# A hybrid decoder layer on one core: how its weight sums, its channel steps and the X of its recurrence are laid out

## Chip, cores and metric

One Trainium2 chip, one of its cores. The time is device microseconds of one execution of the program; the median of three runs of the kernel before is 2164.18 us (2163.83 to 2165.83). TensorE (PE) does the matmuls, VectorE (DVE) and ScalarE (ACT) the elementwise work, GpSimd (POOL) a little arithmetic and the issue of many DMAs, SyncE (SP) the issue of the loads.

## The reference

One decoder layer over 2048 tokens of width 1024, all in float32. A state-space branch and a sliding-window attention branch share one input projection; their outputs are normalised, concatenated and projected; a SwiGLU FFN of hidden width 2816 follows. Cut to what this change touches:

```python
# state-space branch: 32 groups of 16 channels, 64 complex states each
_, _, xr, xi = lax.associative_scan(_s5_combine, (a_re, a_im, bu_re, bu_im), axis=1)
y = (einsum('blgp,ghp->blgh', xr, c_re) - einsum('blgp,ghp->blgh', xi, c_im) + d * uf)
y = gelu(y.reshape(bsz, L, SSM_WIDTH))
...
# FFN
gu = rms_norm(h, g_pre_ffn) @ w_gate_up
ff = (silu(gu[..., :D_FF]) * gu[..., D_FF:]) @ w_down
h = h + rms_norm(ff, g_post_ffn)
```

## The kernel before

The layer runs in three phases: projection with the recurrence (to about 352 us), attention with the output projection (to about 799 us), and the FFN, which takes the rest. A planner orders the instructions of each engine ahead of time from priorities and its own estimate of durations; on the chip each engine then runs its list strictly in that order. Operations handed to `keep_in_program_order` (called `pin` in the channel steps) keep the place that the program gives them.

**Recurrence.** Time is cut into 256 chunks (NC) of 8 steps. `table_quad` (called for four quads) builds the matrices of the groups on chip and stores them in `tab_d`. `ssm_pair` (16 pairs of groups) loads its table `tab` and its input U, makes S with matmuls (L659: for each of two parts r, real and imaginary, and each group g2 of the pair, an output of 64 partitions), turns S into X on DVE (rotation, scan L672, rotation back) and computes Y = Toeplitz part (L686, from U) + state part (L687, from X); gelu (L689) and a store follow. Before, X is held as [part r in the upper or lower 64 partitions, group, chunk], so that four DVE operations of 64 partitions each write it, crossing partitions, and one Y bank takes, for each group, one matmul of 128 rows with U and one of 128 rows with X. Every float32 matmul of these is two instructions in the trace. The PSUM tag "pa" has four banks; S, Y and the transposes of V take theirs from it. The tiles tab have two buffers, those of U, X and y three. `weave` hands out about 0.9 pairs after each group of 24 matmuls of the Q, K and V projection (`qkv_stream`, tile ps_q).

**FFN.** Each half s of the tokens (1024) runs `ffn_gu` and then `ffn_down`. Both use a seven-product scheme for 2x2 blocks, which needs sums of blocks of the activations and of the weights. `gu_runs` gives 21 runs: the first does the column blocks 0 and 11 together, each later one does one block. A run has four steps q, each with some matmuls. After every second run `ff_operands` stores the products F4 and their sums (tile fxd, POOL, L1312 to L1318). F4 has one buffer.

**Weight sums.** `down_sums` is a generator of 48 DMAs on POOL from DRAM to DRAM (L1334, tile wsd, 512 KB each, some that add to what is there), pinned. During the first half, three are handed out at the end of each run.

**Channel steps.** `channel_steps(1, ...)` turns the rows of the second half around for its FFN: `load` (SP, tile hx), `scale` (ACT L1119, pinned), `turn` (eight transposes on PE, L1127, pinned), then in the second four of eight rows also two loads (tile hb) and `sums` (four DVE operations, the first pinned, and four stores, L1154). The tiles hx and hb share one buffer, ho has another. Before, 21 steps are handed out, one at the end of each run, and the load of row i+1 stands in the same step as the last use of row i:

```python
steps += [chain((scale, i)), chain((even, t), (load, i + 1))]
steps += [chain((scale, i)), chain((odd, t)), chain((sums, t), *([(load, i + 1)] if t < 3 else []))]
```

Of the kernel before, what the change touches and what calls it, by code (L numbers as in the profile page):

```python
# [9 lines left out]
F32 = mybir.dt.float32  # L10
# [3 lines left out]
AF = mybir.ActivationFunctionType  # L14
ALU = mybir.AluOpType
# [4 lines left out]
P = 128  # L20
# [11 lines left out]
NC = SEQ // T8  # L32
# [15 lines left out]
class Layer:  # L48
# [448 lines left out]
    def table_quad(self, q):  # L497

        nc, tp = self.nc, self.p_tab
        qs = slice(4 * q, 4 * q + 4)  # L500
        S4 = [P, 4, 16, 8]
        t1 = tp.tile(S4, F32, tag="qt1", name=f"qt1_{q}")
        t2 = tp.tile(S4, F32, tag="qt2", name=f"qt2_{q}")
        gr = tp.tile(S4, F32, tag="qgr", name=f"qgr_{q}")
        gi = tp.tile(S4, F32, tag="qgi", name=f"qgi_{q}")
        rr = self.rwr[:, qs, :].unsqueeze(2).to_broadcast(S4)
        ri = self.rwi[:, qs, :].unsqueeze(2).to_broadcast(S4)
        br = self.bb[:, 0, qs, :].unsqueeze(3).to_broadcast(S4)
        bi = self.bb[:, 1, qs, :].unsqueeze(3).to_broadcast(S4)
        self.cmul(gr, gi, rr, ri, br, bi, t1, t2)  # L510
        yield
        krev = self.bank([P, 4, 32], "krev")
        for i in range(4):
            nc.tensor.matmul(krev[:, i, :], gr[:, i].rearrange("p h j -> p (h j)"),
                             self.cbd[:, 0, 4 * q + i].rearrange("p g h -> p (g h)"), start=True, stop=False)
            nc.tensor.matmul(krev[:, i, :], gi[:, i].rearrange("p h j -> p (h j)"),
                             self.cbd[:, 1, 4 * q + i].rearrange("p g h -> p (g h)"), start=False, stop=True)
        out = tp.tile([P, 4, 768], F32, tag="tabout", name=f"tabout_{q}")
        for r, g in enumerate((gr, gi)):
            w = self.bank([P, 4, P], "ws")  # L520
            for i in range(4):
                nc.tensor.transpose(w[:, i, :], g[:, i].rearrange("p h j -> p (h j)"), self.ident)
            nc.scalar.copy(out[:, :, r * P:(r + 1) * P], w)
        kd = tp.tile([P, 8, 16], F32, tag="kd", name=f"kd_{q}")
        self.tt(kd, self.dmask.unsqueeze(1).to_broadcast([P, 8, 16]),
                self.d_in[:, 8 * q:8 * q + 8].unsqueeze(2).to_broadcast([P, 8, 16]), ALU.mult)
        self.tt(kd, kd, krev.rearrange("p a (g h) -> p (a g) h", g=2), ALU.add)
        yield
        for i2 in range(2):
            tb = self.bank([P, 4, P], "toep")  # L530
            for i in range(4):
                ii = i2 * 4 + i
                nc.tensor.matmul(tb[:, i, :], self.ext[:, ii, :],
                                 kd.rearrange("p g h -> p (g h)"), start=True, stop=True)
            for a in range(4):
                nc.scalar.copy(
                    out[:, a, 256:512].rearrange("p (g i) -> p g i", i=8)[:, :, i2 * 4:i2 * 4 + 4],
                    tb[:, :, a * 32:(a + 1) * 32].rearrange("p i g -> p g i"))
        fr = self.pwr[:, qs, 1:9].unsqueeze(2).to_broadcast(S4)
        fi = self.pwi[:, qs, 1:9].unsqueeze(2).to_broadcast(S4)  # L540
        cr = self.c_in[:, 0, qs, :].unsqueeze(3).to_broadcast(S4)
        ci = self.c_in[:, 1, qs, :].unsqueeze(3).to_broadcast(S4)
        ca = out[:, :, 512:768].rearrange("p q (g h i) -> p q g h i", g=2, h=16)
        self.tt(t1, fr, cr, ALU.mult)
        self.tt(t2, fi, ci, ALU.mult)
        for g2 in range(2):
            s = slice(g2 * 64, g2 * 64 + 64)
            self.tt(ca[0:64, :, g2], t1[s], t2[s], ALU.subtract)
        yield
        self.tt(t1, fr, ci, ALU.mult)  # L550
        self.tt(t2, fi, cr, ALU.mult)
        for g2 in range(2):
            s = slice(g2 * 64, g2 * 64 + 64)
            nc.vector.scalar_tensor_tensor(
                out=ca[64:128, :, g2].rearrange("p q h i -> p q (h i)"),
                in0=t1[s].rearrange("p q h i -> p q (h i)"), scalar=-1.0,
                in1=t2[s].rearrange("p q h i -> p q (h i)"), op0=ALU.mult, op1=ALU.subtract)
        nc.gpsimd.dma_start(self.tab_d[q][:, :, 0:768], out)
        yield

        E = tp.tile([P, 4, 2, NC], F32, tag="tabout", name=f"Etab_{q}")
        nc.scalar.copy(E[:, :, :, 0:64], self.E6[:, qs])
        for m in (64, 128):
            ng = self.tmp([P, 4], tag="eng")
            self.ts(ng, E[:, :, 1, m - 1], -1.0, None, ALU.mult, ALU.bypass)
            for i in range(4):
                et = tp.tile([P, 2, P], F32, tag="et", name=f"et_{q}_{m}_{i}", bufs=2)
                nc.scalar.activation(et[:, :, :m], E[:, i, :, 0:m], AF.Copy, scale=E[:, i, 0, m - 1:m])
                nc.vector.scalar_tensor_tensor(out=E[:, i, 0, m:2 * m], in0=E[:, i, 1, 0:m], scalar=ng[:, i:i + 1],
                                               in1=et[:, 0, :m], op0=ALU.mult, op1=ALU.add)  # L570
                nc.vector.scalar_tensor_tensor(out=E[:, i, 1, m:2 * m], in0=E[:, i, 0, 0:m],
                                               scalar=E[:, i, 1, m - 1:m],
                                               in1=et[:, 1, :m], op0=ALU.mult, op1=ALU.add)
        nc.gpsimd.dma_start(self.tab_d[q][:, :, 768:1280], E.rearrange("p q r c -> p q (r c)"))
        yield
# [71 lines left out]
    def ssm_pair(self, pr):  # L647
        nc = self.nc
        m, r0 = pr // 4, (pr % 4) * 32
        tab = self.s_tab.tile([P, 1280], F32, tag="tab", name=f"tab_{pr}")  # L650
        nc.sync.dma_start(tab, self.tab_d[m][:, pr % 4, :])
        U = self.s_u.tile([P, 2, NC], F32, tag="U", name=f"U_{pr}")
# [21 lines left out]
        b1 = self.s_z.tile(sh, F32, tag="a1", name=f"b1_{pr}")  # L674
        b2 = self.s_z.tile(sh, F32, tag="a2", name=f"b2_{pr}")
        self.tt(b1, z, erb, ALU.mult)
        self.tt(b2, z, eib, ALU.mult)
        X = self.s_u.tile([P, 2, NC], F32, tag="X", name=f"X_{pr}")
        nc.gpsimd.memset(X[:, :, 0:1], 0.0)
        for r, op in ((0, ALU.subtract), (1, ALU.add)):  # L680
            for g2 in range(2):
                s = slice(g2 * 64, g2 * 64 + 64)
                self.tt(X[r * 64:r * 64 + 64, g2, 1:NC], b1[s, r, 0:NC - 1], b2[s, 1 - r, 0:NC - 1], op)
        Y = self.bank([P, 2, NC], "Y")
        for g2 in range(2):
            nc.tensor.matmul(Y[:, g2, :], tab[:, 256 + g2 * P:384 + g2 * P], U[:, g2, :], start=True, stop=False)  # L686
            nc.tensor.matmul(Y[:, g2, :], tab[:, 512 + g2 * P:640 + g2 * P], X[:, g2, :], start=False, stop=True)  # L687
        y = self.s_u.tile([P, 2, NC], F32, tag="y", name=f"y_{pr}")
        nc.scalar.activation(y, Y, AF.Gelu_apprx_tanh)  # L689
        nc.scalar.dma_start(self.yT_d[m][r0:r0 + 32].rearrange("(g h) i c -> (h i) g c", g=2), y)  # L690


# [413 lines left out]
    def channel_steps(self, s, xp, xtag, xbufs, op, otag, obufs, bank):  # L1106

        nc = self.nc
# [47 lines left out]
        def chain(*fs):  # L1156
            return lambda: [f(i) for f, i in fs]

        steps = [chain((load, 8 * s))]
        for t in range(4):  # L1160
            i = 8 * s + t
            steps += [chain((scale, i)), chain((even, t), (load, i + 1))]
        for t in range(4):
            i = 8 * s + 4 + t
# [58 lines left out]
    def ffn_gu(self, s):  # L1223
        nc, tc = self.nc, self.tc
        with ExitStack() as c:
# [11 lines left out]
            for n, fs in enumerate(self.gu_runs()):  # L1237
                if fs[0] < NJ:
                    j = fs[0]
                    F4 = ff.tile([P, 4, TB], F32, tag="f4", name=f"f4_{s}_{j}")  # L1240
                groups = [self.gu_group(s, f, F4, ev) for f in fs]
                for q in range(4):
                    for g in groups:
                        self.gu_ahead()
                        next(g, None)
                    if fs[-1] == NF - 1 and q > 1:
                        self.got.append(self.down_operands(s, 0, q - 2))
                if fs[-1] >= NJ:
                    self.ff_operands(s, j, F4)
                if s == 0:  # L1250
                    for _ in range(3):
                        next(sums, None)
                    if side and n > 0:
                        side.pop(0)()
                    if n == 0:
                        side.pop(0)()
            for f in side:
                f()

    def gu_ahead(self):  # L1260

# [289 lines left out]
```

## Time and profile before

| | |
|---|---|
| median of 3 runs | 2164.18 us |
| profiled execution | 2163.8 us |
| its span (first to last instruction) | 2162.0 us |
| mean granted TensorE clock | 0.974 of full |
| PE busy | 2017.5 us (93%) |
| DVE busy | 1388.7 us (64%) |
| ACT busy | 924.4 us (43%) |
| POOL busy | 301.3 us (14%) |

PE is busy for most of the span, so time is to be had only where PE waits or runs at less than its full clock, or by giving it less to do. Busy shares are averages over stages; the stages around the change are read one by one. Idle time printed behind an instruction is that of its engine just before it, with what ended it.

### The profile page before, as it was taken

How to read it: one execution, taken by the hardware profiler on the slowest of the kernel's cores; microseconds unless marked ns; L12 is line 12 of the kernel's file. 1: busy time of each engine (PE TensorE's matmuls, PEld its weight loads, DVE VectorE, ACT ScalarE, POOL GpSimd, SP SyncE). 2: the span in 40 equal slices, each digit the busy share in tenths (PEclk: the TensorE clock that was granted, in tenths of full speed). 3: DMA queues.
4: the chain of work that ended last, by engine and by line, in shares of the span. 5: the costliest groups of instructions: out<-in, count | busy, mean ns of one | idle time of the engine just before them, and what ended most of it. 6: DMA issues, size and time to landing. Idle time of an engine off the chain costs nothing. (4 is left out here: it accounts for less than half of the span.)

```text
span 2162.0 us, 25798 instructions
## 1 busy us (share of the span) xinstructions
PE 2017.5 (93%) x9200; PEld 1635.8 (76%) x9200; DVE 1388.7 (64%) x2199; ACT 924.4 (43%) x1469; POOL 301.3 (14%) x655
## 2 busy tenths in 40 slices
PE   7998987999999798999979999999899999999997
PEld 5777665887877686778768777887688888887885
DVE  7876887887676747565456565446766656554446
ACT  6433114976565454333233344435333333334443
POOL 3211000112223431212112110001000000000001
PEclk9999998999899999999999999999999999999998
DMA  8566656534246744667566466656423222256664
GB/s 280 209 229 204 187 151 180 153 101 154 81 152 202 265 156 162 243 173 221 161 200 171 165 244 219 191 192 229 161 103 127 93 107 103 83 175 224 204 195 175
DMA packets 177425, 379.73 MB, mean 176 GB/s; under 512 B 32864, under 2 KB 53856, under 8 KB 177104
## 3 DMA queue, kind: packets, MB, share of 16 engines
q1 hardware_dynamic: 138112, 259.89, 37.6%
q0 software_dynamic: 32512, 109.79, 15.5%
q10 hardware_dynamic: 6672, 8.40, 1.3%
q8 instruction: 72, 1.18, 0.2%
q14 instruction: 57, 0.47, 0.1%
HBM read 281.87 MB, written 119.21 MB: 186 GB/s over the span
## 5 line engine op out<-in xcount | busy, mean ns | idle before, releaser
L220 PE MATMUL ps_gb<-bh,wh 128*128 128x512 f32 x704 | 279.4, 398 | 14.6 <-ACT f L1289 7.4
L222 PE MATMUL ps_gb<-bh,wl 128*128 128x512 f32 x704 | 275.6, 393 | 8.7 <-DVE wl L172 8.7
L221 PE MATMUL ps_gb<-bl,wh 128*128 128x512 f32 x704 | 277.0, 393 | 0.0
L222 PE MATMUL ps_dn<-wh_d,wl_x 128*128 128x512 f32 x616 | 244.3, 398 | 8.1 <-DVE wl_x L172 6.1
L220 PE MATMUL ps_dn<-wh_d,wh_x 128*128 128x512 f32 x616 | 243.6, 395 | 6.0 <-ACT wh_x L1091 4.2
L221 PE MATMUL ps_dn<-wl_d,wh_x 128*128 128x512 f32 x616 | 243.4, 395 | 1.1 <-DVE wl_d L172 1.1
L220 PEld LDWEIGHTS ps_gb<-bh,wh 128*128 128x128 f32 x704 | 133.3, 190 | 51.6 <-ACT f L1289 10.4
L222 PEld LDWEIGHTS ps_gb<-bh,wl 128*128 128x128 f32 x704 | 133.1, 189 | 39.4 <-DVE wl L172 10.0
L221 PEld LDWEIGHTS ps_gb<-bl,wh 128*128 128x128 f32 x704 | 133.1, 189 | 28.2 <-DVE bl L172 0.2
L220 PE MATMUL ps_gc<-bh,wh 128*128 128x512 f32 x352 | 139.8, 398 | 13.0 <-ACT wh L171 10.6
L171 ACT CAST wh<-fr 128x1024 fp32r<-128x1024 f32 (+1 forms) x88 | 73.5, 835 | 171.8 <-issue 87.9
L222 PEld LDWEIGHTS ps_dn<-wh_d,wl_x 128*128 128x128 f32 x616 | 117.7, 192 | 36.6 <-DVE wl_x L172 8.9
L220 PEld LDWEIGHTS ps_dn<-wh_d,wh_x 128*128 128x128 f32 x616 | 117.9, 191 | 32.2 <-ACT wh_x L1091 5.5
L172 DVE TENSOR_TENSOR wl_x<-xr,wh_x 128x1024 fp32r<-128x1024 f32 x72 | 81.6, 1133 | 92.4 <-ACT wh_x L171 92.4
L222 PE MATMUL ps_gc<-bh,wl 128*128 128x512 f32 x352 | 139.2, 396 | 0.5 <-DVE wl L172 0.5
L221 PE MATMUL ps_gc<-bl,wh 128*128 128x512 f32 x352 | 139.3, 396 | 0.0
L221 PEld LDWEIGHTS ps_dn<-wl_d,wh_x 128*128 128x128 f32 x616 | 117.8, 191 | 26.1 <-DVE wl_d L172 1.6
L172 DVE TENSOR_TENSOR wl_d<-dr,wh_d 128x1024 fp32r<-128x1024 f32 x84 | 95.1, 1132 | 61.1 <-ACT wh_d L171 61.1
L171 ACT CAST wh_x<-xr 128x1024 fp32r<-128x1024 f32 x72 | 70.7, 982 | 123.2 <-PE ps_dn L221 116.2
L171 ACT CAST wh_d<-dr 128x1024 fp32r<-128x1024 f32 x84 | 82.4, 981 | 91.1 <-PE ps_dn L221 64.0
L76 DVE TENSOR_TENSOR q<-ps_ga,q 128x512 f32<-128x512 f32 x44 | 30.3, 689 | 111.9 <-PE ps_ga L222 111.5
L172 DVE TENSOR_TENSOR wl<-sb,wh 128x1024 fp32r<-128x1024 f32 x44 | 53.8, 1222 | 61.5 <-ACT wh L171 61.5
(368 smaller groups left out, 4624.6 us busy)
## 6 DMA issues: line engine op xcount, KB each, us to landing
fr<-in_w_gu SPq DMA_DIRECT2D x88, 512.0 KB
xr<-fxd SPq DMA_DIRECT2D x70, 512.0 KB
dr<-wsd SPq DMA_DIRECT2D x40, 512.0 KB
fxd<-f POOLq DMA_DIRECT2D x22, 768.0 KB, 4.8
gwr_o<-in_w_out SPq DMA_DIRECT2D x64, 256.0 KB
wsd<-in_w_down POOLq DMA_DIRECT2D x30, 512.0 KB, 10.3
dr<-in_w_down SPq DMA_DIRECT2D x30, 512.0 KB
raw<-in_xT SPq DMA_DIRECT2D x56, 256.0 KB
```

The source lines that it names most:

```text
L76: (eng or self.nc.vector).tensor_tensor(out=out, in0=a, in1=b, op=op)
L171: nc.scalar.copy(hi, x)
L172: nc.vector.tensor_tensor(out=lo, in0=x, in1=f32(hi), op=ALU.subtract)
L220: t.matmul(out, wh, mh, start=first, stop=False, skip_group_check=more)
L221: t.matmul(out, wh, ml, start=False, stop=False, skip_group_check=more)
L222: t.matmul(out, wl, mh, start=False, stop=last, skip_group_check=more)
```

## The change

Three edits. In `table_quad` and `ssm_pair` X and its matrix are held by groups: the partitions are those of the states (group, state), and the free axis has the part r. Two DVE operations of 128 partitions write X; Y gets a bank for each group, with one matmul of 128 rows from U and two matmuls of 64 rows (partitions 0 to 63 for the first group, 64 to 127 for the second) from X; gelu runs once for each bank. In `ffn_gu` one weight sum goes out after step q = 0, one after q = 2 and one at the end of a run; the channel steps are handed out at q = 1 and q = 3 of all runs but the first. In `channel_steps` of the second half a load is a step of its own with an empty step behind it, and so is `odd`: 40 steps in place of 21.

```diff
         qs = slice(...)                       # table_quad
-        ca = out[:, :, 512:768].rearrange("p q (g h i) -> p q g h i", g=2, h=16)
+        ca = out[:, :, 512:768].rearrange("p q (r h i) -> p q r h i", r=2, h=16)
-        for g2 in range(2):
-            s = slice(g2 * 64, g2 * 64 + 64)
-            self.tt(ca[0:64, :, g2], t1[s], t2[s], ALU.subtract)
+        self.tt(ca[:, :, 0], t1, t2, ALU.subtract)
...
-        for g2 in range(2):
-            s = slice(g2 * 64, g2 * 64 + 64)
-            nc.vector.scalar_tensor_tensor(out=ca[64:128, :, g2]..., in0=t1[s]..., scalar=-1.0, in1=t2[s]...)
+        nc.vector.scalar_tensor_tensor(out=ca[:, :, 1]..., in0=t1..., scalar=-1.0, in1=t2...)
...
         for r, op in ((0, ALU.subtract), (1, ALU.add)):     # ssm_pair
+            self.tt(X[:, r, 1:NC], b1[:, r, 0:NC - 1], b2[:, 1 - r, 0:NC - 1], op)
+        Y = [self.bank([P, NC], "Y") for _ in range(2)]
+        for g2 in range(2):
+            nc.tensor.matmul(Y[g2], tab[:, 256 + g2 * P:384 + g2 * P], U[:, g2, :], start=True, stop=False)
+        for r in range(2):
             for g2 in range(2):
                 s = slice(g2 * 64, g2 * 64 + 64)
-                self.tt(X[r * 64:r * 64 + 64, g2, 1:NC], b1[s, r, 0:NC - 1], b2[s, 1 - r, 0:NC - 1], op)
-        Y = self.bank([P, 2, NC], "Y")
+                nc.tensor.matmul(Y[g2], tab[s, 512 + r * P:640 + r * P], X[s, r, :], start=False, stop=r == 1)
+        y = self.s_u.tile([P, 2, NC], F32, tag="y", name=f"y_{pr}")
         for g2 in range(2):
-            nc.tensor.matmul(Y[:, g2, :], tab[:, 256 + g2 * P:384 + g2 * P], U[:, g2, :], start=True, stop=False)
-            nc.tensor.matmul(Y[:, g2, :], tab[:, 512 + g2 * P:640 + g2 * P], X[:, g2, :], start=False, stop=True)
-        y = self.s_u.tile([P, 2, NC], F32, tag="y", name=f"y_{pr}")
-        nc.scalar.activation(y, Y, AF.Gelu_apprx_tanh)
+            nc.scalar.activation(y[:, g2], Y[g2], AF.Gelu_apprx_tanh)
...
+        if s:                                                # channel_steps
+            steps = []
+            for t in range(4):
+                i = 8 * s + t
+                steps += [chain((load, i)), chain(), chain((scale, i)), chain((even, t))]
+            for t in range(4):
+                i = 8 * s + 4 + t
+                steps += [chain((load, i)), chain(), chain((scale, i)), chain((odd, t)), chain(), chain((sums, t))]
+            return steps
...
+                    if q % 2 == 0:                           # ffn_gu, in the loop over q
+                        next(sums, None)
+                    elif side and n > 0:
+                        side.pop(0)()
                 if fs[-1] >= NJ:
                     self.ff_operands(s, j, F4)
-                if s == 0:
-                    for _ in range(3):
-                        next(sums, None)
-                    if side and n > 0:
-                        side.pop(0)()
-                    if n == 0:
-                        side.pop(0)()
+                next(sums, None)
             for f in side:
                 f()
+            for _ in sums:
+                pass
```

## Rows read from the trace of the kernel before

**Rows 1.** The page, busy time of the engines, share of the span, instructions.

```profile
PE 2017.5 (93%) x9200; PEld 1635.8 (76%) x9200; DVE 1388.7 (64%) x2199; ACT 924.4 (43%) x1469; POOL 301.3 (14%) x655
```

**Rows 2.** Waits of PE, 850 to 1265 us: total, times, longest.

```profile
PE ps_gc L220 <- ACT wh L171: 8.2, 1, 8.2
PE ps_gb L220 <- ACT f L1289: 7.4, 5, 2.8
PE ps_gb L220 <- ACT wh L171: 3.9, 3, 1.4
```

**Rows 3.** Stretches: length, busy PE, PEld, DVE, ACT, POOL, granted clock, DMA.

```profile
200.00:352.00 152.00, 127.34 (x563) 91.09 (x561) 127.42 (x239) 27.26 (x53) 12.47 (x35) 0.94 0.59 170
...
280.00:290.00 10.00, 10.00 (x50) 7.71 (x49) 9.87 (x20) 1.85 (x5) 0.10 (x1) 1.00 0.40 124
```

**Rows 4.** Groups of DVE, 200 to 352 us: busy, mean ns, idle before.

```profile
L76 DVE TENSOR_TENSOR X<-b,b 64x255 f32<-64x255 f32 x64 | 26.8, 419 | 1.6
L76 DVE TENSOR_TENSOR a<-ps_S,tab 128x512 f32<-128x512 f32 x32 | 21.1, 686 | 18.2 <-PE ps_S L659 17.9
...
L76 DVE TENSOR_TENSOR a<-a,a 128x256 f32<-128x256 f32 x32 | 12.1, 419 | 0.3
```

**Rows 5.** Groups of PE in the same stretch.

```profile
L659 PE MATMUL ps_S<-U,tab 128*64 128x256 f32 x128 | 22.0, 427 | 19.3 <-DMA U<-uTd 6.6 <-issue 6.3 <-DMA tab<-tabd 6.2
L687 PE MATMUL ps_Y<-X,tab 128*128 128x256 f32 x64 | 21.7, 424 | 4.8 <-DVE X L76 4.7
```

**Rows 6.** Timeline of one pair: start us, us, engine, line, operation.

```profile
250.32 0.39 PE L220 MATMUL ps_q<-xs,wh 128*128 128x512 f32 x1
...
250.77 1.08 PE L659 MATMUL ps_S<-U,tab 128*64 128x256 f32 x8
251.60 1.73 DVE L76 TENSOR_TENSOR X<-b,b 64x255 f32<-64x255 f32 x4
...
251.78 0.70 PE L686 MATMUL ps_Y<-U,tab 128*128 128x256 f32 x2
...
253.53 0.60 PE L686 MATMUL ps_Y<-U,tab 128*128 128x256 f32 x2
...
253.97 0.59 PE L687 MATMUL ps_Y<-X,tab 128*128 128x256 f32 x2
...
258.07 1.73 DVE L76 TENSOR_TENSOR X<-b,b 64x255 f32<-64x255 f32 x4
```

**Rows 7.** Groups of ACT, 200 to 352 us.

```profile
L689 ACT ACTIVATE y<-ps_Y 128x512 f32<-128x512 f32 x16 | 9.6, 598 | 65.9 <-PE ps_Y L687 61.0 <-DMA yTd<-y 4.9
...
L619 ACT COPY qe<-ps_q 128x512 f32<-128x512 f32 x6 | 3.5, 586 | 24.2 <-PE ps_q L222 12.2 <-DMA qd<-qe 9.8 <-DMA kd<-qe 2.2
```

**Rows 8.** The tile tabout, its DVE writes: ns min/median/max, first and last start.

```profile
L76 DVE TENSOR_TENSOR tabout<-qt,qt x8: 674/684/691, 89.5 to 174.6; 64x512 f32<-64x512 f32 x8
```

**Rows 9.** Timeline around the longest wait of the FFN's first half.

```profile
1111.99 2.50 POOL L1334 DMA_DIRECT2D wsd<-wsd  x5
1112.44 0.33 SPq L1116 DMA_DIRECT2D hx<-hd  x1
...
1127.22 1.15 ACT L1119 ACTIVATE hx<-hx,rstd 128x1024 f32<-128x1024 f32 x1 [8.64 <-DMA wsd<-wsd]
```

**Rows 10.** Timeline of PE behind that wait.

```profile
1129.88 0.79 PE L220 MATMUL ps_gc<-bh,wh 128*128 128x512 f32 x1 [8.21 <-ACT wh L171]
...
1133.03 0.41 PE L222 MATMUL ps_gb<-bh,wl 128*128 128x512 f32 x1
1133.27 0.40 PE L220 MATMUL ps_gb<-bh,wh 128*128 128x512 f32 x1
```

**Rows 11.** Timeline around a later row of the channel steps.

```profile
1235.43 0.34 SPq L1116 DMA_DIRECT2D hx<-hd  x1
...
1242.35 1.15 ACT L1119 ACTIVATE hx<-hx,rstd 128x1024 f32<-128x1024 f32 x1 [2.81 <-DMA hx<-hd]
```

**Rows 12.** The stretch of the twenty later runs of the FFN's first half.

```profile
864.00:1270.00 406.00, 386.14 (x1694) 311.49 (x1693) 234.06 (x323) 137.62 (x185) 75.26 (x102) 0.99 0.63 188
```

More of the change, by code (lines that the diff above doesn't have):

```diff
@@ L551, in table_quad @@
         self.tt(t2, fi, cr, ALU.mult)
-        for g2 in range(2):
-            s = slice(g2 * 64, g2 * 64 + 64)
[L554 to L557, printed above, removed]
+        nc.vector.scalar_tensor_tensor(
+            out=ca[:, :, 1].rearrange("p q h i -> p q (h i)"),
+            in0=t1.rearrange("p q h i -> p q (h i)"), scalar=-1.0,
+            in1=t2.rearrange("p q h i -> p q (h i)"), op0=ALU.mult, op1=ALU.subtract)
         nc.gpsimd.dma_start(self.tab_d[q][:, :, 0:768], out)
```

## The prediction

> **What bounds the kernel now.** The page comes first: PE is busy for 93% of the span, DVE for 64% [rows 1]. So a microsecond taken off DVE, POOL or a queue counts only where PE waits for it, and the question for each edit is which wait of PE stands behind it. The three edits touch two stages, which the waits of PE and the stretches take apart.
>
> The first half of the FFN (about 864 to 1270 us) is bound by PE, with few waits. From 850 to 1265 us the large ones are one of 8.2 us for a split of weights on ACT, five of together 7.4 us for a copy on ACT and three of together 3.9 us for splits again [rows 2]. The 8.2 us can be followed: POOL issued five weight sums within 2.5 us from 1111.99 on, SP issued a load hx at 1112.44, and ACT started the scaling of that row only at 1127.22, after 8.64 us in which it did nothing [rows 9]. The scaling is pinned, ACT runs in order, and the split that PE needed stood behind it. PE then began below its full clock: its eight matmuls from 1129.88 to 1133.03 took 3.15 us, where at the pace from 1133.03 to 1133.27 they take 1.9 [rows 10]. That is 1.2 us more.
>
> The recurrence (200 to 352 us, 16 pairs, 9.5 us each) has no single bound: PE and DVE are each busy for 127 of 152 us [rows 3]. Where DVE runs without gaps, one X follows the last by 6.47 us (251.60 to 258.07) [rows 6]. Nine of the fifteen 10-us stretches from 200 to 350 have DVE at 9.2 us or more, of which one is shown [rows 3]; in the others DVE waits for S, 17.9 us in all [rows 4], and PE for U, tab and issue, 19.1 us [rows 5]. tab is loaded again only when the Y of two pairs before is done, so this wait is a loop through X, Y and a load.
>
> **X by groups, DVE.** 64 writes of 64 partitions become 32 of 128. The old take 419 ns; so do operations of 128 partitions and 256 elements [rows 4], so the new are taken at 419 as well: 64 x 0.419 = 26.8 us become 13.4. If all of it shortens the stage it is -13.4. It is taken at the share of stretches that DVE fills, 9 of 15: -8.0 us. In the rest the waited-for load starts a little earlier too, which is counted at nothing.
>
> **X by groups, PE.** Per pair four instructions of 128 rows become eight of 64 rows; the Toeplitz part keeps four. The old pace is (253.97 - 253.53) / 2 = 0.22 us [rows 6], so 64 x 0.22 = 14.1 us now. No row has matmuls of 64 rows. The nearest is S, whose halves go to different partitions of the output: eight in 1.01 us (250.77 to 251.78), 0.126 each, so two run side by side there [rows 6]. By S: 128 x 0.126 = 16.1 us, +2.0. With no pair side by side: 128 x 0.22 = 28.2, +14.1. I take S, since the two groups use different rows and different banks.
>
> Going into S also costs: the matmul before starts 0.45 us ahead of it, where a full pace is 0.24 [rows 6, 10], so 0.2 us is lost. The new matmuls stand between ones of full height, two changes per pair, 32 x 0.22 = 7.0 us. Together +9.1 us of PE, between +2.0 and +21.1.
>
> The Trainium skill, page "TensorEngine Tiling (Array Packing)", section "Key Properties", says that changing the tiling mode drains the engine; the gap ahead of S agrees with it. The same section says that tiles work independently. By both rules the sum would be +9.1, without the first +2.0.
>
> PE idles for 25 of 152 us, which covers most of that. Only where PE is full as well does it lengthen the stage; that is so in three of the fifteen stretches, as in the one shown [rows 3]: 9.1 x 3/15 = +1.8 us. Without that cover it costs the 9.1. The stage gives -8.0 + 1.8 = -6.2 us, between -13.4 and about 0. Gelu in two pieces costs ACT a fixed part more; ACT is busy for 27 of 152 us [rows 3], so nothing.
>
> **The table.** Sixteen DVE writes of 64 partitions, 0.684 us [rows 8], become eight: 5.5 us of DVE over four quads, 1.4 each. Quads wait for their stores and, at the end, for an ACT copy that stood behind a store. Counted at nothing, at best -1.4 (the last quad).
>
> **Weight sums and channel steps.** Twenty runs take 406 us, 20.3 each, of which PE is busy for 386 [rows 12]. Work and number of DMAs stay; only the order changes. The sums come one at a time, some 5 to 10 us apart. A load of the channel steps moves from the step of the sums, where on SP it waits for the stores out of the same buffer, to half a run later, and keeps a whole run until its scaling. Behind it on SP stand weight loads, which lose a blocker. Between scaling and transposes half a run is left, 10 us; pinned transposes on PE would wait if ACT were later than that, but ACT is lightly used. The three sums that now go out in the first run pass POOL's stores of h and arithmetic there; nothing on PE waits for those for a whole run, so nothing, at most +2.
>
> With no burst in front, a load needs about what it needed at 1235.43, where the scaling followed at 1242.35, 6.9 us later [rows 11]; 20 us cover it. So the 8.2 and the 1.2 us go. The 2.81 us that ACT waited at 1242.35 cost PE the longest of the five copy waits, 2.8 us [rows 2, 11]; there the load was issued late, behind the stores, and half a run of distance removes that. The other four (7.4 - 2.8 = 4.6, with the 3.9 us of splits) come from the order on ACT, and may fall otherwise: I add one more such pair, 4.6/4 + 3.9/3 = +2.5 us. Sum: -8.2 - 1.2 - 2.8 + 2.5 = -9.7 us. Bounds: -12.2 without new waits, 0 if the waits only move.
>
> **Sum.** 2163.8 (profiled) - 6.2 - 9.7 = 2147.9 us. The profiled execution is 0.4 us below the median of the runs, so 2148 us.
>
> **The rivals.**
> *PE fills the recurrence.* If 64-row matmuls do not run side by side, PE gets +21.1 on 127.3 us, 148 of 152, and takes over as the bound: the stage stays, and 2163.8 - 9.7 = 2154. For it: no row shows such matmuls. Against: S.
> *The bursts stay.* The sums are pinned on POOL, in a list that also has stores waiting for DVE; a wait there can collect the single sums into a burst again, so that the edit doesn't do what it says. Then only the recurrence gains: 2163.8 - 6.2 = 2158. For it: three sums are handed out per run, yet five went in one stretch [rows 9]. Against: with one per step at most two should collect.
> *Neither gains*: both of these, 2164.
> *The banks run out (slower).* A pair takes three of the four "pa" banks instead of two, and a Toeplitz part made early holds them. If S of the next pair must wait for the gelu, DVE idles for every pair: X chain 6.47 - 0.84 = 5.6, Y 1.0, change 0.2, gelu 0.6 [rows 7], S 1.0, and the queue of PE ahead of S, say eight projection matmuls of 0.24 = 1.9: 10.3 us per pair, (10.3 - 9.5) x 16 = +13. ACT's waits for stores, 9.8 us at L619 [rows 7], then hold banks too. 13 + 9.8 - 9.7 = +13: 2177. It decides from 9.5 + 9.7/16 = 10.1 us per pair. For it: with Y made early, four banks leave no spare. Against: S waits for tab anyway, which comes after that Y.
> The skill's page on tiling, section "Restrictions and Gotchas", names the same pressure: row tiles write to different PSUM banks. No run here shows it yet.
>
> **How the numbers follow.** A measurement of this kernel can tell 0.2%, 4.3 us, from no change. The forecast has 0.45 (its own range 2140 to 2156), PE filling 0.18, bursts 0.12, neither 0.10, banks 0.15. Faster: 0.45 + 0.18 + most of 0.12 (0.09) = 0.72. Same: 0.03 + 0.10 = 0.13. Slower: 0.15. The range begins where both stages reach their best bound (-13.4 - 1.4 - 12.2 = -27: 2137) and ends at 2168, past "neither"; what lies beyond is most of the banks' 0.15.
>
> **What would show it.** X: 32 writes of 128x255 near 0.42 us. Y from X: 64-row matmuls at about 0.13 us from start to start (0.22 means the first rival). The last Y some 6 us earlier. The 8.2 us wait gone, no scaling waiting over 1 us, sums singly on POOL. S waiting for ACT's gelu, or pairs over 10.1 us, means the banks. The prediction is wrong if the planner, given other durations, moves waits elsewhere: attention and the second FFN half, which the edits don't touch, should be within 3 us.

## The result, and the profile after

The changed kernel is slower: 2179.95 us, median of six runs (2174.89 to 2184.96), against 2165.01 us for the kernel before (2163.37 to 2171.32); the ratio is 1.0066, 95% interval 1.0044 to 1.0087. The forecast was 2148 us with a range of 2137 to 2168. The profiled execution of the changed kernel, 2174.89 us, is the shortest of its six, so the stages below add up to less than the medians differ by.

First the stages, cut where PE starts the last ps_u, the first ps_z, the first ps_gb and the first ps_dn of its timeline (us; the profiled executions, spans 2162.0 and 2173.1):

| stage | before | after | difference |
|---|---|---|---|
| start to last ps_u | 119.4 | 122.6 | +3.2 |
| recurrence, to first ps_z | 234.8 | 229.9 | -4.9 |
| attention and mixer, to first ps_gb | 444.9 | 449.4 | +4.5 |
| FFN, first half, to first ps_dn | 471.2 | 486.4 | +15.2 |
| the rest | 891.7 | 884.7 | -7.0 |

The recurrence gains and attention gives it back; the first half of the FFN, where 9.7 us were to go, loses 15.2. Of the rest, -6.1 us lie in the first half's down product, which took anything from 223 to 229 us in the kernels below; no edit touches it, and most of the difference is clock: in it PE was at the lower of its two granted levels for 17.1 us in the trace of before and for 3.4 in that of after.

**The FFN's first half.** Waits of PE in the changed kernel, 850 to 1290 us (total, times, longest), to be set against [rows 2]:

```profile
PE ps_gb L220 <- ACT f L1296: 15.2, 7, 3.4
PE ps_gc L220 <- ACT wh L171: 4.7, 1, 4.7
PE ps_gb L220 <- ACT wh L171: 4.2, 4, 1.4
```

The 8.2 us are gone, but the waits for the copy f have doubled, from 7.4 us to 15.2. Four of the seven are alike; this is the timeline of the first of them:

```profile
881.28 0.39 PE L222 MATMUL ps_gc<-bh,wl 128*128 128x512 f32 x1
881.70 0.59 ACT L1299 COPY q<-ps_gc 128x512 f32<-128x512 f32 x1 [4.01 <-PE ps_gc L222]
882.18 1.15 ACT L1117 ACTIVATE hx<-hx,rstd 128x1024 f32<-128x1024 f32 x1
883.24 1.06 ACT L1296 COPY f<-ps_gb 128x512 f32<-128x512 f32 x2
883.86 0.50 PE L220 MATMUL ps_gb<-bh,wh 128*128 128x512 f32 x1 [2.20 <-ACT f L1296]
...
884.75 0.63 PE L220 MATMUL ps_gb<-bh,wh 128*128 128x512 f32 x1
...
888.30 0.39 PE L220 MATMUL ps_gb<-bh,wh 128*128 128x512 f32 x1
```

ACT had nothing to do for 4.01 us, then copied ps_gc, then scaled hx for 1.15 us, and only then copied ps_gb, for which PE stood. The row had been loaded long before (the load was issued at 865.01). So PE waits 2.20 us, which is the 1.16 us of the undisturbed hand-over (as at 1118.63 us in the trace of before) and 1.04 of the scaling. And the wait has a tail: from 884.75 PE's matmuls start 0.43 us apart in place of 0.23, until 888.

Such stretches at half pace are a large part of the loss. The granted clock tells how long they last:

```profile
884.75:888.00 3.25, 3.25 (x9) 2.56 (x8) 2.28 (x4) 1.35 (x2) 0.00 (x0) 0.51 0.04 16
```

(Length, busy PE, PEld, DVE, ACT, POOL, granted clock, DMA.) Over the first half PE was at this lower level for 13.7 us in the trace of before and for 34.1 in that of after. At half pace half of that time is lost, so the difference costs 10.2 us; 3.4 of the 20.4 us more lie ahead of 850 us, where no channel step is at work yet. The waits of PE grow by 3.7 us (29.7 to 33.3). Together that is 13.9 of the 15.2.

GpSimd shows the other thing. Its waits in the same stretch:

```profile
POOL bTd L1138 <- DVE ho L76: 101.3, 4, 33.5
POOL bTd L1133 <- DVE ho L76: 99.1, 3, 34.1
POOL bTd L1152 <- DVE hb L1147: 72.2, 3, 31.2
...
POOL fxd L1319 <- DVE f L76: 22.7, 3, 19.4
```

In the kernel before the long waits were those of F4's store:

```profile
POOL fxd L1312 <- DVE f L76: 156.5, 9, 32.1
```

There L1138's and L1133's counterparts stood at 60.0 and 45.5 (longest 20.0 and 16.6). POOL now waits for ho, with F4's store and the single sums behind it in its list. What comes then is seen in the timeline around 1180 us:

```profile
1177.16 0.71 POOL L1152 DMA_DIRECT2D bTd<-ho  x1 [16.87 <-DVE ho L76]
1177.89 0.72 POOL L1152 DMA_DIRECT2D bTd<-hb  x1
1178.52 0.84 POOL L1319 DMA_DIRECT2D fxd<-f  x1
...
1180.74 3.70 POOL L1341 DMA_DIRECT2D wsd<-in_w_down  x4
1181.20 0.33 SPq L1114 DMA_DIRECT2D hx<-hd  x1
1183.49 1.08 ACT L1296 COPY f<-ps_gb 128x512 f32<-128x512 f32 x2 [3.33 <-DMA fxd<-f]
...
1190.73 1.15 ACT L1117 ACTIVATE hx<-hx,rstd 128x1024 f32<-128x1024 f32 x1 [6.17 <-DMA hx<-hd]
...
1193.39 0.80 PE L220 MATMUL ps_gc<-bh,wh 128*128 128x512 f32 x1 [4.66 <-ACT wh L171]
```

It is the picture of [rows 9] again: four sums in one go, a load of hx beside them, ACT waiting for it, PE waiting for ACT. New is that F4's store comes so late that ACT has to wait 3.33 us before it may write F4 again.

**The recurrence.** The groups that answer to [rows 4] and [rows 5], 200 to 352 us (busy, mean ns, idle before):

```profile
L76 DVE TENSOR_TENSOR X<-b,b 128x255 f32<-128x255 f32 x32 | 12.0, 418 | 0.6
...
L684 PE MATMUL ps_Y<-X,tab 64*128 64x256 f32 x128 | 19.1, 417 | 5.5 <-DVE X L76 5.5
```

X takes half of its DVE time. PE's idle time ahead of S goes from 19.3 us to 13.9:

```profile
L655 PE MATMUL ps_S<-U,tab 128*64 128x256 f32 x124 | 18.4, 406 | 13.9 <-ACT xs L171 4.4 <-DMA tab<-tabd 3.9 <-issue 3.7
```

On PE the timeline of one pair:

```profile
253.00 1.13 PE L684 MATMUL ps_Y<-X,tab 64*128 64x256 f32 x8
...
254.22 1.08 PE L655 MATMUL ps_S<-U,tab 128*64 128x256 f32 x8
```

From the first of the eight to S are 1.22 us here, of which 0.08 are a wait for tab. Instruction by instruction, the eight start in twos 0.216 us apart, 0.108 for each, so two do run side by side. In eleven of the sixteen pairs the next matmul follows 0.31 us after the eighth, with no wait, where a full pace is 0.22: a change costs about 0.1 us. The last group of Y starts at 327.2 us (before: 350.4). But PE's last product of the projection for Q, K and V now starts at 348, after the last Y; before it started at 344, ahead of it.

### The profile page after: what moved, and what is told of

Same layout as the page of the kernel before. It is cut to its first block, busy times and chain, and to the rows that moved or that the text cites. A ratio compares the mean times of both kernels' runs of the same rounds, so it can differ in the third digit from the quotient of the medians.

```text
span 2173.1 us, 25905 instructions
## 1 busy us (share of the span) xinstructions
PE 2032.2 (94%) x9264; PEld 1642.5 (76%) x9264; DVE 1369.7 (63%) x2159; ACT 927.6 (43%) x1484; POOL 303.9 (14%) x655
## 4 chain that ended last, share of the span: by engine, by line
PE 45%; issue 26%; DVE 8%; DMA 8%; POOL 3%; ACT 3%; SPq 0%; DVEq 0%; POOLq 0%; ACTq 0%
PE ps_dn L222 5%; PE ps_dn L221 5%; PE ps_dn L220 5%; PE ps_gb L220 3%; PE ps_gb L222 3%; PE ps_gb L221 2%; PE ps_wo L220 2%; DMA hr<-bTd 2%; PE ps_wo L222 2%; PE ps_wo L221 2%; PE ps_gc L220 1%; PE ps_gc L221 1%; PE ps_gc L222 1%; PE ps_O L870 1%; PE ps_O L869 1%
## 5 line engine op out<-in xcount | busy, mean ns | idle before, releaser
L220 PE MATMUL ps_gb<-bh,wh 128*128 128x512 f32 x704 | 284.3, 405 | 24.3 <-ACT f L1296 16.1
L222 PE MATMUL ps_gb<-bh,wl 128*128 128x512 f32 x704 | 280.3, 400 | 8.8 <-DVE wl L172 8.8
L76 DVE TENSOR_TENSOR f<-ps_gc,f 128x512 f32<-128x512 f32 x44 | 30.4, 691 | 97.9 <-ACT f L1296 58.8
```

The source lines that it names most:

```text
L76: (eng or self.nc.vector).tensor_tensor(out=out, in0=a, in1=b, op=op)
L220: t.matmul(out, wh, mh, start=first, stop=False, skip_group_check=more)
L222: t.matmul(out, wl, mh, start=False, stop=last, skip_group_check=more)
```

## The experiments

Stage lengths are those of the table above, from one profiled execution each; the ratio is to the kernel before, measured beside it, with its 95% interval.

| kernel | ratio | recurrence | attention | FFN, first half |
|---|---|---|---|---|
| before | 1 | 234.8 | 444.9 | 471.2 |
| after | 1.0066 (1.0044 to 1.0087) | 229.9 | 449.4 | 486.4 |
| x_only | 0.9999 (0.9978 to 1.0021) | 233.9 | 451.9 | 474.4 |
| sums_only | 0.9992 (0.9971 to 1.0013) | 235.8 | 444.6 | 470.3 |
| steps_only | 1.0037 (1.0015 to 1.0058) | 234.0 | 443.2 | 482.4 |
| ffn_both | 1.0038 (1.0016 to 1.0060) | 239.5 | 445.3 | 485.1 |
| scale_q0 | 1.0023 (1.0007 to 1.0039) | 228.9 | 452.6 | 480.2 |
| turn_end | 1.0040 (1.0025 to 1.0054) | 232.5 | 451.4 | 479.7 |
| both_moved | 1.0004 (0.9988 to 1.0019) | 226.5 | 452.7 | 474.6 |
| x_rate | 1.0006 (0.9990 to 1.0021) | 230.7 | 451.9 | 475.0 |
| x_lead5 | 1.0007 (0.9989 to 1.0024) | 231.7 | 458.4 | 475.1 |
| x_split | 1.0025 (1.0010 to 1.0039) | 237.5 | 455.3 | 475.2 |
| both_lead5 | 0.9989 (0.9975 to 1.0004) | 233.5 | 459.9 | 473.0 |
| sums_early | 0.9958 (0.9942 to 0.9974) | 228.3 | 453.9 | 464.7 |
| early_before | 0.9927 (0.9905 to 0.9950) | 236.2 | 446.4 | 460.2 |
| early_noX | 0.9965 (0.9949 to 0.9980) | 236.5 | 446.4 | 465.9 |
| after_early | 0.9981 (0.9965 to 0.9997) | 228.3 | 452.2 | 470.9 |

### Each part by itself

**x_only** is the kernel before with the edits of `table_quad` and `ssm_pair`, the first blocks of the diff above.

> Only the X by groups (table and pairs), weight sums and channel steps as before. Theory A (the loss sits in the FFN's first half, in the channel steps handed out inside the runs): this kernel is between 2158 and 2167 us, since the projection ends about 2 us earlier and attention gives that back. Theory B (the single weight sums cost the time): the same here. Theory C (the 64-row matmuls, or the three banks of a pair, cost it): 2172 us or more, with the FFN starting over 8 us later than before.

**sums_only** hands out the sums as the change does and keeps the old channel steps, one a run:

```diff
+                    if q % 2 == 0:
+                        next(sums, None)
...
-                if s == 0:
-                    for _ in range(3): next(sums, None)
+                next(sums, None)
```

> Only the weight sums one at a time (after q = 0, q = 2 and at the end of a run); X, list and place of the channel steps as before. Theory A: 2155 to 2167 us; sums no longer come six in a row, because stores of ho stay behind the stores of F4 on POOL. Theory B: 2172 us or more. Theory C: no change, 2162 to 2167.

**steps_only** has the new channel steps at q = 1 and 3 and the old bursts:

```diff
+                    if q % 2 and side and n > 0:
+                        side.pop(0)()
...
                     for _ in range(3): next(sums, None)
```

> Only the channel steps: the new list with empty steps, handed out at q = 1 and q = 3; three sums at the end of a run and X as before. Theory A: 2172 to 2185 us; POOL waits over 20 us several times for ho ahead of the store of F4, and PE waits 2.2 us for the copy of f behind the scaling, about four times. Theory B: 2160 to 2167. Theory C: 2160 to 2167.

**ffn_both** has both edits of the FFN and the old X.

> Sums and channel steps as after the change, X as before. Theory A: 2172 to 2185 us, close to steps_only. Theory B: 2172 or more, close to sums_only. Theory C: 2160 to 2167.

Neither X nor the single sums do anything that can be measured by themselves; in sums_only the wait of 8.2 us is gone and one of 5.7 stands at the same load. The channel steps carry the loss of the FFN, 1.0037 alone and 1.0038 with the sums; their first half takes 482.4 and 485.1 us, where after has 486.4. The ratio of after is larger, 1.0066. It differs from ffn_both in X alone, and x_only shows no loss; 0.0028 is about the width of the two intervals, and what it is stays open.

### Two places of the channel steps

The loss could lie in where the scaling stands on ACT (between the copies), or in where ho's stores stand on POOL (ahead of F4's), or in neither. Two kernels move one of them each, a third both:

```diff
-                    elif side and n > 0:                 # scale_q0
+                    if q in (0, 3) and side and n > 0:
...
-                    elif side and n > 0:                 # turn_end
+                    if q == 1 and side and n > 0:
...
                 next(sums, None)
+                if side and n > 0:
+                    side.pop(0)()
```

both_moved has `q == 0` and the step at the run's end.

> The changed kernel with its channel steps handed out at q = 0 and 3 of a run in place of q = 1 and 3: the scaling of hx now stands in ScalarE's list ahead of the copy of ps_gc, where ScalarE was idle (4.01 us before that copy at 881.70), and no longer between it and the copy of ps_gb; ho's stores stay ahead of F4's store in GpSimd's list. Theory A1 (the scaling between the two copies costs): TensorE's waits for f by the copy fall from 2.20 to about 1.2 us and the half-clock matmuls behind them go, four times 1.0 + 2 us: the first half of the FFN takes 474 to 477 us instead of 486.5, ratio to before about 1.001 to 1.002. Theory A2 (ho's stores in front of F4's store and of the sums on GpSimd cost): nothing moves here, 484 to 487 us, ratio 1.005 to 1.007.

> The changed kernel with the second channel step of a run handed out at the run's end, behind ff_operands, in place of q = 3: F4's store then stands ahead of ho's stores in GpSimd's list; the scaling stays at q = 1, between the two copies. Theory A2: GpSimd's waits for ho no longer hold F4's store, ScalarE does not wait for the DMA of fxd, the sums go out in smaller groups, and the first half of the FFN takes 478 to 481 us instead of 486.5, ratio about 1.002 to 1.004. Theory A1: the 2.20 us waits stay, 482 to 486 us, ratio 1.004 to 1.006.

> The changed kernel with both moves: one channel step at q = 0, the other at the run's end behind ff_operands. If A1 and A2 are the whole loss, the first half of the FFN is back at 468 to 472 us and, with X by groups costing nothing, the ratio to before is 0.997 to 1.001. If the loss lies in something else (the sums one at a time beside the loads, or the banks), it stays at 480 us or more, ratio above 1.004.

In scale_q0 the timeline that answers to 881.28 above reads

```profile
878.36 1.14 ACT L1117 ACTIVATE hx<-hx,rstd 128x1024 f32<-128x1024 f32 x1
882.46 0.59 ACT L1299 COPY q<-ps_gc 128x512 f32<-128x512 f32 x1 [2.97 <-PE ps_gc L222]
882.95 1.08 ACT L1296 COPY f<-ps_gb 128x512 f32<-128x512 f32 x2
883.59 0.50 PE L220 MATMUL ps_gb<-bh,wh 128*128 128x512 f32 x1 [1.16 <-ACT f L1296]
```

The scaling runs in what was ACT's idle time, and PE waits 1.16 us and keeps its pace. Of the four waits of 2.20 us one is left, at 1127.42, where the scaling still stands between the two copies. The stage takes 480.2 us, not the 474 to 477 put down: the waits beside the late loads, 4.76 us the longest, are still there. In turn_end, F4's store is again what POOL waits for (waits of POOL, 850 to 1285 us):

```profile
POOL fxd L1321 <- DVE f L76: 115.7, 7, 30.4
POOL bTd L1138 <- DVE ho L76: 60.9, 4, 19.7
POOL bTd L1133 <- DVE ho L76: 46.4, 3, 18.4
```

Both moves count: the ratio goes from 1.0066 to 1.0023, to 1.0040, and with both to 1.0004. Against both_moved, measured beside them, the scaling is worth 3.6 thousandths and ho's stores 1.9, the latter about the width of the intervals; against after, measured in another series, 4.3 and 2.6. In the traces each move alone takes 6 to 7 us off the stage, and both take 11.8. The first half of the FFN is at 474.6 us, not the 468 to 472 expected: waits for a late load are still there, the longest 5.96 us. The timeline in both_moved around it:

```profile
1112.28 0.72 POOL L1152 DMA_DIRECT2D bTd<-ho  x1 [13.71 <-DVE ho L76]
1113.00 0.73 POOL L1152 DMA_DIRECT2D bTd<-hb  x1
1113.63 1.14 POOL L1343 DMA_DIRECT2D wsd<-wsd  x2
...
1116.55 0.33 SPq L1114 DMA_DIRECT2D hx<-hd  x1
1116.91 1.55 POOL L1343 DMA_DIRECT2D wsd<-wsd  x3
...
1125.58 1.15 ACT L1117 ACTIVATE hx<-hx,rstd 128x1024 f32<-128x1024 f32 x1 [3.67 <-DMA fxd<-tb]
...
1127.25 0.79 PE L220 MATMUL ps_gb<-bh,wh 128*128 128x512 f32 x1 [5.96 <-ACT f L1298]
```

The load is issued 3.55 us after the store of hb, out of whose buffer it writes; in the kernel before that was 3.26 (1109.18 to 1112.44), in the changed one 3.31 (1177.89 to 1181.20). The store lands at 1116.49, 1112.38 and 1181.15, each time some 0.05 us ahead of the load. So these loads start when that store has landed, wherever the step of the load stands: the empty step behind it gives them no time. (The five loads ahead of them wait for no store of hb and were early enough in either kernel: 15 to 30 us from issue to scaling, and ACT waited for none.) And right there the sums go out.

### When the sums are done

**sums_early** is both_moved with four sums a run in place of three, so that POOL has issued the last of the 48 (at 1092.53) ahead of the first store of hb (1104.20); **early_before** is the kernel before with four (1086.86 and 1098.59):

```diff
-                    if q % 2 == 0:                       # sums_early
+                    if q < 3:
                         next(sums, None)
...
-                    for _ in range(3):                   # early_before
+                    for _ in range(4):
                         next(sums, None)
```

**after_early** is the changed kernel with `q < 3` for its sums, its channel steps staying at q = 1 and 3 (its last sum goes out at 1113.24, behind the first store of hb at 1108.47, but ahead of the first load that waits for one); **early_noX** is sums_early with the old X.

> The kernel both_moved with the sums one at a time but four in a run in place of three, so that all are issued ahead of the first store of hb and none beside the sixth load of hx (which in both_moved took from 1116.55 to 1125.58, with 2 sums ahead of it, F4's three stores around it and 4 sums behind it). If the sums draw the load out: the load lands in 4 to 6 us, TensorE's wait of 5.96 us at 1127 falls to under 3, the first half of the FFN 469 to 472 us, ratio 0.997 to 0.999. Rival: F4's stores alone, or the load's late issue (it waits for the store of hb in the same buffer), keep the wait: 474 us, ratio 1.000 to 1.002.

> The kernel before with four weight sums handed out at each run's end in place of three, still together, its channel steps and X as they were: all sums are issued ahead of the first store of hb, so none stands beside the three loads of hx that wait for hb's store. If it is sums beside those loads that made TensorE's 8.21 us wait: the wait falls under 3, the first half of the FFN takes 460 to 464 us in place of 471, ratio 0.995 to 0.997; then neither the empty step nor the handing out one at a time was needed. Rival: without them the wait keeps 5 us or more, 468 to 472 us, ratio 0.999 to 1.001.

> The kernel sums_early with X of the recurrence as before. It differs from sums_early in X by groups alone. If X by groups gains in its stage what attention loses by its other order: recurrence stage about 235 us (sums_early 228), attention and mixer 443 to 445 us (sums_early 454), ratio to before 0.994 to 0.997, within 0.002 of sums_early's 0.9958. If X by groups really gains 3 to 5 us, this kernel is slower than sums_early, at 0.998 or more.

> The changed kernel, channel steps at q = 1 and 3 as they are, with four sums a run in place of three. The scaling still stands between the two copies, and ho's stores ahead of F4's. Theory: these two losses do not depend on the sums, so the 2.20 us waits stay, while the waits of 4.66 and 3.36 us beside the late loads go: the first half of the FFN 476 to 481 us in place of 486.5, ratio 1.001 to 1.004. Rival: the loss lay in the sums held back behind ho's stores: 465 to 470 us, ratio 0.996 to 0.998.

One number in the kernel before does more than the whole change: early_before is faster by 0.73% (0.50 to 0.95), 2153.01 us against 2166.81, and the fastest of all. From 850 us on the FFN's first half has no wait of PE over 1.3 us there. The load behind the 8.21 us wait of the kernel before is the one at 1118.79 here: from its issue to its scaling are 7.5 us, of which ACT waited 1.4, where the same load took 14.8 beside five sums in the kernel before [rows 9] and 9.0 in both_moved. ACT's order at this place is the same as in the kernel before, though the planner changed it elsewhere. The next load, at 1159.69 with no store of F4 beside it, takes 4.8 us, where the changed kernel's took 9.5 beside four sums and F4's stores. Of the 8.21 us PE still waits 1.29. Over the stage PE's waits fall from 29.7 to 19.2 us and the time at the lower clock from 13.7 to 10.2, together 12.2 of lost time against a gain of 11.0. sums_early tells the same of both_moved: the wait of 5.96 us is gone and the stage takes 464.7 us, better than the 469 to 472 put down. Timeline of early_before at the late loads:

```profile
1115.51 0.72 POOL L1154 DMA_DIRECT2D bTd<-hb  x1
...
1118.79 0.33 SPq L1116 DMA_DIRECT2D hx<-hd  x1
...
1124.96 0.50 PE L220 MATMUL ps_gb<-bh,wh 128*128 128x512 f32 x1 [1.16 <-ACT f L1289]
1126.29 1.15 ACT L1119 ACTIVATE hx<-hx,rstd 128x1024 f32<-128x1024 f32 x1 [1.38 <-DVE sa L76]
...
1129.29 0.50 PE L220 MATMUL ps_gc<-bh,wh 128*128 128x512 f32 x1 [1.29 <-ACT wh L171]
...
1159.69 0.33 SPq L1116 DMA_DIRECT2D hx<-hd  x1
...
1164.53 1.15 ACT L1119 ACTIVATE hx<-hx,rstd 128x1024 f32<-128x1024 f32 x1 [4.66 <-DMA hx<-hd]
```

The sums still go out in bursts there, and the channel steps have no empty step. That early_noX, with its sums spread out and its steps apart, takes 465.9 us where early_before takes 460.2 says that the new order costs something even then (3.7 us more of PE's waits, 3.4 us more at the lower clock); which part was not tried. after_early did better than expected, 470.9 us where 476 to 481 were put down, and nearer to its rival. With the sums early and nothing else changed, 15.5 us come back, as much as the whole loss. So what the channel steps lose they lose for the larger part together with the sums, and the gains of the single moves do not add up. Its four 2.20 us waits are there, but only two of them are followed by the half pace; this is one of the other two:

```profile
887.85 0.50 PE L220 MATMUL ps_gb<-bh,wh 128*128 128x512 f32 x1 [2.20 <-ACT f L1296]
...
890.26 0.39 PE L221 MATMUL ps_gb<-bl,wh 128*128 128x512 f32 x1
```

### Where X's gain goes

**x_split** is x_only with each write of X in two halves, as many DVE instructions as before; **x_rate** is x_only with fewer turns for the recurrence beside the projection; **x_lead5** and **both_lead5** are x_only and both_moved with attention started one step less ahead.

```diff
-            self.tt(X[:, r, 1:NC], b1[:, r, 0:NC - 1], b2[:, 1 - r, 0:NC - 1], op)      # x_split
+            for o in (0, 64):
+                h = slice(o, o + 64)
+                self.tt(X[h, r, 1:NC], b1[h, r, 0:NC - 1], b2[h, 1 - r, 0:NC - 1], op)
...
-        self.rs = 0.9                                                                   # x_rate
+        self.rs = 0.75
...
-        self.lead = 6                                                                   # x_lead5, both_lead5
+        self.lead = 5
```

> X by groups alone, each of its writes split in two of 64 partitions, so that VectorE writes X in 64 instructions as before, while TensorE keeps the 64-row matmuls and the two Y banks. By the prediction's sum VectorE's part (-8.0 in the stage) goes and TensorE's (+1.8) stays: from the last ps_u to the first ps_z about 240 us in place of 229 to 234, ratio to before 1.003 to 1.004. Rival: the stage ends with the Q/K/V projection and not with VectorE, so that 64 or 32 writes are the same: 229 to 235 us, ratio 0.999 to 1.001.

> X by groups alone, with the recurrence given 0.75 steps instead of 0.9 for each step of the Q/K/V projection that it is woven with. If the stage's gain is lost because the recurrence, now shorter, finishes 20 us ahead and leaves the projection's end alone before attention: the last projection product ends 2 to 4 us earlier than at 0.9 and the attention and mixer stage goes back from 450 to 452 us to about 445, total 2158 to 2162 us, ratio 0.996 to 0.998. Rival: what attention gave back has another cause (the order of VectorE's work there): 450 us again, ratio 0.999 to 1.001.

> X by groups alone, with attention's lead 5 in place of 6: TensorE's list from the first ps_z to the first ps_gb then nearly follows the order of the kernel before (the runs of one tile's name match it to 0.92; in every kernel with X by groups so far to 0.77, in every one without it to 1.00). Theory: the recurrence stage's gain of 3 to 5 us is real and lost because the planner, seeing the recurrence end earlier, orders attention otherwise: from the first ps_sc to the first ps_gb 443 to 445 us again in place of 448, total ratio 0.996 to 0.998. Rival: the 5 us belong to X by groups itself (later Q rows at attention's start): 447 to 449 us, ratio 0.999 to 1.001.

> The kernel both_moved with lead 5. If what remains of the loss is attention's order, 3 to 5 us go: ratio to before 0.997 to 0.999, the first half of the FFN at 472 to 475 us as in both_moved. Rival: ratio 1.000 to 1.001.

x_split puts the recurrence back to 237.5 us, but it does not show that the gain is DVE's, for it changed PE's part too: its 64-row matmuls no longer run two at a time. In one pair eight of them and the change behind take 1.89 us (254.57 to 256.46; in after mostly 1.07), and the group from 200 to 352 us is busy for 29.0 us, where that of after has 19.1:

```profile
L686 PE MATMUL ps_Y<-X,tab 64*128 64x256 f32 x128 | 29.0, 452 | 1.6 <-DVE X L76 1.2
```

So x_split took back both parts at once, and no run takes back one alone. Over the six traces without X by groups (before among them) that stage takes 236.1 us in the mean (234.0 to 239.5), over the eight with it, whole and at lead 6, 229.9 (226.5 to 233.9): -6.2 us. PE's waits in it fall from 29.0 to 22.6 us, the time at the lower clock from 23.5 to 17.9 (2.8 us of lost time), and what is left, PE's own work, grows by 3. So the gain is no gain of PE's work; that the waits are shorter because of DVE is likely, not shown. Attention goes the other way, 445.1 (443.2 to 446.4) against 452.0 (449.4 to 453.9): +6.9. The ratios say the same, 0.9999 for x_only, and 0.9958 against 0.9965 for sums_early and early_noX, which differ in X alone (after and ffn_both, as said, differ the other way). X by groups is worth nothing here that can be measured.

Two things can be seen behind it, read from the traces and not tested apart. The last ps_q starts 226.2 us after the last ps_u in the mean without X and 225.3 with it, while the last Y goes from 232.5 to 204.3: with X by groups the projection ends the stage, and attention waits for Q (in the trace of after 6.9 us for QS, eight times; before 4.0, three times), so that at the first ps_sc 4.2 of the 6.2 us are left. And the planner orders attention otherwise: written down as stretches of matmuls into tiles of one name, PE's order there is the same in all kernels without X and another in all with it. From the first ps_sc to the first ps_gb it takes 448.1 us in the mean in place of 443.2; PE's waits there are 39.1 us in place of 34.9, and those for QS alone 8.0 in place of 4.0. x_rate did not bring the projection forward: its last ps_q starts 225.8 us after the last ps_u, 3.7 earlier than in x_only but where the other kernels with X have it, and its ratio is that of its rival. Lead 5 brought the order nearer to the old one but not the time; its two profiled executions lie 11 and 12 us above their medians, so its stages are no evidence, and its ratios, 1.0007 and 0.9989, show no gain. What in the new order makes PE wait longer for QS stays open.

## Why the prediction failed, point by point

**X on DVE and on PE: the sum came out, its working only in part.** -8.0 and +1.8 were put down, -6.2 together, and -6.2 is the difference of the means. That it agrees to the tenth is luck: the kernels spread over 7 us, and 2.8 of the 6.2 are clock. The times of the new DVE writes, 418 ns, and the 64-row matmuls side by side came as forecast, and no S waits for a gelu in the trace of after (one does in x_only, 1.2 us); so the rivals of a full PE and of the banks fell. The price on PE was too high: eight matmuls and the changes on both sides cost some 1.2 us a pair, 0.3 more than the old four, where the +9.1 us of the prediction make it 0.57. Its 0.2 us for a change was read where PE also waited 0.06 us for U; without a wait it is 0.1. The rule of the Trainium skill that a change of the tiling mode drains the engine ("TensorEngine Tiling (Array Packing)", "Key Properties") agrees with this 0.1 us. "The last Y some 6 us earlier" was wrong: it came 23 us earlier (350.4 to 327.2), and the stage now ends with the projection, which the prediction did not see as a bound.

**That attention would stay within 3 us: wrong.** The prediction named the planner as what could break it, and gave it no chance and no price. Attention became 6.9 us longer in the mean, which took all of X's gain.

**"With no burst in front, a load needs about what it needed at 1235.43 ...; 20 us cover it": wrong, and this is the step that failed.** It stands behind the -8.2, the -1.2 and the -2.8 of the sum, -9.7 us where +15.2 were measured. It took two things for granted. One is that a load handed out half a run later is issued then, with the stores that it waits for done. It is issued when the store of hb has landed, and that store waits in POOL's list for DVE: the load at 1181.20 was issued 0.05 us after the landing, and ACT stood 6.17 us for it. The other is that the burst would be gone: four sums went out in one go at 1180.74. With the sums early and the channel steps as they are, the stage is back at 470.9 us. *The bursts stay* was a rival at 0.12, with the right mechanism, stores that wait for DVE; but it was priced as no gain, and the change itself put more of these stores ahead: ho's, for which POOL stands up to 34 us.

**"ACT is lightly used": true and no help.** ACT was idle before the copies and is busy for a third of the time. What counted was the place in its list: 1.15 us between two copies for which PE waits, at four loads of eight. The prediction allowed +2.5 us for "one more such pair" of waits. The four cost 4 x 1.04 = 4.2 us, and three of them about 1.6 us of half pace each (eight matmuls 0.2 us longer); moving the scaling, for three of the four, gained 6.2 us in the trace, 8 to 9 us by the ratios (0.0036 to 0.0043 x 2165).

**The clock.** It was taken as something that leaves with the 8.2 us wait (-1.2; by the granted clock, 0.50 for the 3.15 us, it was 1.6). It came back with other waits, +10.2 us, the larger part of the loss.

**The gain was there, elsewhere.** The prediction read [rows 9] rightly, sums beside a load. It costed spreading the sums and moving the load, not having the sums done before the load: that gains 0.73% with one number.

## What to carry to other kernels

Ask of a step that is handed out earlier not when its turn comes but what its first instruction waits for: here a load waited for a store out of the same buffer, so that moving its step did not make it start earlier, while clearing the queues at the moment when it does start gained 0.7% (in the kernel before). On engines that run a fixed list, a short instruction off the critical path is dear if it lands between two that the bound engine waits for; read the neighbours in the list, not the busy share. A gain of a stage is to be followed to the next hand-over: X saved 6 us of the recurrence and the total did not move.

## What the runs showed of the hardware

In the first half of the FFN from 850 us on, over all seventeen traces, 119 waits of PE of 1.0 to 1.4 us were followed by no stretch at half pace. Of 19 waits of 2.1 to 2.3 us, 13 were followed by a fall of the granted clock within 1.5 us of PE's going on, and by matmuls 0.43 us apart. The length of the wait is not all: at the start of the stage, where PE has more waits, one of 1.43 us was followed by such a fall in four of the seventeen. Granted clock in two stretches of the changed kernel, the second with such a wait (length, busy PE, PEld, DVE, ACT, POOL, granted clock, DMA):

```profile
870.00:880.00 10.00, 10.00 (x46) 8.29 (x45) 4.06 (x6) 2.69 (x4) 4.81 (x8) 1.00 0.99 340
880.00:890.00 10.00, 7.71 (x26) 5.49 (x25) 4.68 (x7) 5.85 (x8) 0.00 (x0) 0.83 0.61 208
```

The 0.83 is a mean of the two levels, 2.4 and 1.2 GHz; the matmuls 0.43 us apart ran at the lower (0.51 from 884.75 to 888.00, above). One microsecond more of waiting thus cost about 2.6 where the pace fell (1.04 and eight times 0.2). Why it did not in six of the 19 is not known.
